# One wide and one narrow matmul per weight tile in the up-projection's paired products, with the halves of a sum added by transfers

## The chip, the cores and the metric

The kernel runs on one core of one Trainium2 chip. The metric is the device time of one execution in microseconds (us), as the median of several runs. The core has five engines that run on their own and meet at semaphores: TensorE (PE, matrix products into PSUM, its weight loads shown apart as PEld), VectorE (DVE), ScalarE (ACT), GpSimd (POOL) and SyncE (SP), which issues most DMA transfers. POOL issues the transfers that add onto their destination.

## The reference

A decoder layer over 512 tokens with 2048 features, all in float32: a token mixer (a recurrent half and an attention half), a layer norm, then a gated MLP with a causal convolution of width 3 over the tokens, then a second layer norm. The part that matters here is the MLP's first half:

```python
x = _layernorm(DEEPNORM_ALPHA * x + mix, ln_mix_g[i], ln_mix_b[i])
hu = _causal_dwconv(jnp.einsum('bsd,df->bsf', x, w_up[i]), ffn_conv_w[i], ffn_conv_b[i])
g, u = jnp.split(hu, 2, axis=-1)                       # 5632 columns each
ffn = jnp.einsum('bsf,fd->bsd', jax.nn.gelu(g) * u, w_down[i])
x = _layernorm(DEEPNORM_ALPHA * x + ffn, ln_ffn_g[i], ln_ffn_b[i])
```

## The kernel before, in words

Features lie on the 128 partitions and tokens along the free dimension, so a product of weights with activations is a sum over tiles of 128 input features. To keep float32 precision with a rounded float32 type (`F32R`), each operand is split into a high part, written by ACT, and a low part, the rest, written by DVE (`split`, lines 106 to 112). A product then needs three matmuls, high x high, high x low and low x high, which all add into one bank (`mm3`, line 114; its matmul is line 117).

The up-projection's 44 column pairs (one tile of g, one of u) are computed in two ways. The first four are plain. The other 40 (class `Pair`, from line 767) use a seven-product scheme: the input features are cut into two halves of eight tiles, the tokens into two halves of 256, and the sums and differences of weights and of activations are formed such that seven products take the place of eight. `PRODUCTS` (line 69) gives their order: p1, p5, p6, p2, p7, p3, p4. Each is a sum over eight tiles of 128 features, of 256 tokens, with three matmuls per tile.

The activation side of the products is built once. `x1[k][h]` holds the normed input of feature tile k and token half h, its high part in the first 256 columns and its low part in the last 256. `forms(j)` (line 727) builds t1 to t4 from sums and differences on POOL, then splits two at a time.

The weight side is loaded per pair. `Pair.before` (line 788) loads four tiles, adds a tile from HBM onto one of them twice with an accumulating transfer (`onto`, line 777, its issue is line 780), adds two sums on DVE (lines 800 and 811) and splits each product's weights two products ahead of its use (lines 110 and 111). `Pair.early` (line 830) copies or adds the finished banks into `cg` and `cu`, 512 columns each: five copies by ACT (lines 835, 838, 840, 845, 850) and three operations by DVE (lines 842, 847, 848). `Pair.late` (line 852) runs the convolution: a scaled copy by ACT (`tap`, line 754), two multiply-adds on DVE (line 748), gelu on ACT (line 862), the product of g and u on DVE (line 866) and a store (line 868).

The loop from line 916 runs one product per step and calls these parts at fixed distances from a pair's first product: a pair's step 0 is its first product, step 6 its last, step 7 the next pair's first. A scheduler then puts each engine's instructions in an order by when their inputs are ready in its own reckoning, so an instruction may stand earlier or later than its call. Tiles come from pools with a fixed number of buffers: `A_BUFS` (62) tiles of 512 columns for all that lives long, `T_BUFS` (12) for the short-lived ones, `RAW_UP` (6) for loaded weights and `W_BUFS` (3) for split ones. Each pair takes three banks of PSUM.

Of the kernel before, what the change touches and what calls it, by code (L numbers as in the profile page):

```python
# [10 lines left out]
F32 = mybir.dt.float32  # L11
F32R = mybir.dt.float32r
AF = mybir.ActivationFunctionType
ALU = mybir.AluOpType
# [33 lines left out]
NC_ = C_LQ + 4 * DH  # L48


A_BUFS = 62
T_BUFS = 12
RAW_BUFS = 3
RAW_UP = 6
# [22 lines left out]
def f32(ap):  # L77
    return ap.bitcast(F32)
# [3 lines left out]
def trunk_kernel(ctx, tc, xT, w_qkg, w_v, gate_w, w_out0, w_out, w_up0, w_up, w_down, consts, out):  # L82
# [11 lines left out]
    def bank():  # L94
        return psum.tile([P, S], F32, tag="ps", bufs=8, name="ps")

    def a_tile(dt=F32R, name="a"):
        return act.tile([P, S], dt, tag="a", bufs=A_BUFS, name=name)

# [6 lines left out]
    def split(src, hi=None, lo=None, mk=a_tile):  # L106

        hi = mk(F32R, "hi") if hi is None else hi
        lo = mk(F32R, "lo") if lo is None else lo
        nc.scalar.activation(hi, src, AF.Copy)  # L110
        nc.vector.tensor_tensor(lo, src, f32(hi), ALU.subtract)  # L111
        return hi, lo

    def mm3(ps, w, x, first, last, onto=False):

        for n, (a, b) in enumerate(((w[0], x[0]), (w[0], x[1]), (w[1], x[0]))):
            nc.tensor.matmul(  # L117
                ps, a, b, start=first and n == 0, stop=last and n == 2, skip_group_check=onto
            )


# [163 lines left out]
    def v_proj(n):  # L285
        pv = [bank() for _ in range(QB)]
        if n == 0:
            load_x(0)
            W.load(1)
            load_x(1)  # L290
            W.load(2)
            load_x(2)
            load_x(3)
            W.load(3)
        for unit in range(KT // 2):
            if n == 0:
                x[2 * unit] = split(x[2 * unit])
            parts = W.take()
            if n + unit == 0:
                parts += W.take()  # L300
            if n == 0:
                x[2 * unit + 1] = split(x[2 * unit + 1])
                load_x(2 * unit + 4)
                load_x(2 * unit + 5)
            for i in range(2):
                kt = 2 * unit + i
                for tt in range(QB):
                    xs = [z[:, tt * P : (tt + 1) * P] for z in x[kt]]
                    mm3(pv[tt], xs, parts[i], kt == 0, kt == KT - 1)
                tick(4 * TK)  # L310
            if n == 0 and unit == 0:
                nc.sync.dma_start(cst, consts)
            if n == 0 and unit == 4:
                constants()
        for tt in range(QB):
            vt[tt] = split(pv[tt])

    def proj():

# [305 lines left out]
    for dt in range(KT):  # L625

        if dt == 3:
            W.hold = True
        if W.hold and not W.raws:
            assert not side  # L630
            early.close()
            W.pool = ctx.enter_context(tc.tile_pool(name="rawu", bufs=1))
            W.bufs, W.hold = RAW_UP, False
            W.load()
        xr = t_tile(F32, "xr")
        nc.sync.dma_start(xr, xT[dt])
        xrs.append(xr)
        if dt == 0:
            continue
        if dt == 1:  # L640
            pair = [bank(), bank()]
            for u in range(KT // 4):
                parts = W.take()
                for kk in range(4):
                    i = 4 * u + kk
                    tick(2 * TK)
                    assert ms[i] is not None
                    hi, lo = parts[kk // 2]
                    for o in range(2):
                        c = slice((kk % 2 * 2 + o) * P, (kk % 2 * 2 + o + 1) * P)  # L650
                        mm3(pair[o], (hi[:, c], lo[:, c]), ms[i], i == 0, i == KT - 1)
            for o in range(2):
                residual(o, pair[o])
            continue
        if dt >= KT - 2:
            wl.append([W.take(), W.take()])
            ys.append(a_tile(F32, "y"))
            continue
        ps = bank()
        for n in range(2):  # L660
            parts = W.take()
            for kk in range(8):
                i = n * 8 + kk
                hi, lo = parts[kk // 4]
                c = slice((kk % 4) * P, (kk % 4 + 1) * P)
                mm3(ps, (hi[:, c], lo[:, c]), ms[i], i == 0, i == KT - 1)
        residual(dt, ps)
# [28 lines left out]
    def sides(z):  # L696
        return z[:, :HALF], z[:, HALF:]
# [29 lines left out]
    def forms(j):  # L727
        a, b = ys[j], ys[j + KT // 2]
        sub = nc.gpsimd.tensor_tensor
        t14, t23 = t_tile(F32, "t14"), t_tile(F32, "t23")  # L730
        (t1, t4), (t2, t3) = sides(t14), sides(t23)
        (b11, b12), (b21, b22) = sides(a), sides(b)
        sub(t1, b12, b11, ALU.subtract)
        sub(t2, t1, b22, ALU.subtract)
        sub(t4, t2, b21, ALU.add)
        sub(t3, b22, b12, ALU.subtract)
        h14, l14 = a_tile(F32R, "hi"), a_tile(F32R, "lo")
        nc.scalar.activation(h14, t14, AF.Copy, scale=-1.0)
        nc.vector.scalar_tensor_tensor(l14, t14, -1.0, f32(h14), ALU.mult, ALU.subtract)
        h23, l23 = split(t23)  # L740
        form["p1", j], form["p2", j] = sides(x1[j][0]), sides(x1[j + KT // 2][0])
        form["p3", j] = sides(x1[j + KT // 2][1])
        form["p5", j], form["p4", j] = zip(sides(h14), sides(l14))
        form["p6", j], form["p7", j] = zip(sides(h23), sides(l23))

    def conv(t, src, ti, *ds):
        for d in ds:
# [19 lines left out]
    class Pair:  # L767
# [49 lines left out]

        def product(self, at):
            if at == 0:
                self.x, self.y, self.z = [bank()[:, :HALF] for _ in range(3)]  # L820
            name = PRODUCTS[at]
            ps = {"p5": self.y, "p3": self.y, "p2": self.z}.get(name, self.x)
            new = name in ("p1", "p5", "p2")
            hi, lo = self.w.pop(name)
            n = KT // 2
            for j in range(n):
                c = slice(j * P, (j + 1) * P)
                mm3(ps, (hi[:, c], lo[:, c]), form[name, j], new and j == 0, j == n - 1, not new)

        def early(self, at):  # L830
            copy, add = nc.scalar.activation, nc.vector.tensor_tensor
            a, b = slice(0, HALF), slice(HALF, S)
            if at == 1:
                self.cg = a_tile(F32, "cg")
                copy(self.cg[:, a], self.x, AF.Copy)
            elif at == 2:
                self.p5 = t_tile(F32, "p5")[:, :HALF]
                copy(self.p5, self.y, AF.Copy)
            elif at == 3:
                copy(self.cg[:, b], self.x, AF.Copy)  # L840
            elif at == 4:
                add(self.cg[:, a], self.cg[:, a], self.z, ALU.add)
            elif at == 5:
                self.cu = a_tile(F32, "cu")
                copy(self.cu[:, b], self.x, AF.Copy, scale=-1.0)
            elif at == 6:
                add(self.cg[:, b], self.cg[:, b], self.y, ALU.add)
                add(self.cu[:, b], self.cu[:, b], self.p5, ALU.subtract)
            elif at == 7:
                copy(self.cu[:, a], self.x, AF.Copy, scale=-1.0)  # L850

        def late(self, at):
            if at == 6:
                self.g = tap(self.cg, 2 * self.i)
                conv(self.g, self.cg, 2 * self.i, 1)
            elif at == 7:
                conv(self.g, self.cg, 2 * self.i, 2)
                self.u = tap(self.cu, 2 * self.i + 1)
            elif at == 8:
                conv(self.u, self.cu, 2 * self.i + 1, 1)  # L860
            elif at == 9:
                nc.scalar.activation(self.g, self.g, AF.Gelu_apprx_tanh)
            elif at == 10:
                conv(self.u, self.cu, 2 * self.i + 1, 2)
            elif at == 11:
                nc.vector.tensor_tensor(self.g, self.g, self.u, ALU.mult)
            elif at == 12:
                nc.sync.dma_start(hidd[self.i], self.g)

    pairs = [Pair(i) for i in range(PLAIN, FT)]  # L870
# [45 lines left out]
    for k in range(last):  # L916
        step(k, "early", 1, 8)
        step(k, "before", -6, 5)
        step(k, "late", 6, 13)
        step(k, "product", 0, NP)  # L920
        ready({last - 5: 4, last - 3: 12, last - 2: 16}.get(k, 0))
        if k == last - 4:
            W.load()
    for k in range(last, last + 6):
        step(k, "early", 1, 8)
        step(k, "late", 6, 13)

    def down_blocks():
        while True:
# [155 lines left out]
```

## Time and profile before

| | |
|---|---|
| median of 3 runs | 2112.58 us (2111.98 to 2113.05) |
| the profiled execution | 2112.73 us |
| its span, first to last instruction | 2111.0 us |
| PE busy | 2076.4 us, 98% |
| DVE, ACT, POOL busy | 63%, 48%, 11% |
| DMA | 286.67 MB, mean 136 GB/s |

The span is what the trace covers; the 1.7 us to the execution's time lie around it. Busy times overlap, since the engines work side by side. PE's busy time counts the pipelined ends of its matmuls too, so how fast it works is read from the distance between starts.

### The profile page before, as it was taken

Reading aid. Unit: us, or ns where it says so; the run is one execution under the profiler, and the core shown is the slowest. Engines: PE = TensorE matmul, PEld = TensorE weight load, DVE = VectorE, ACT = ScalarE, POOL = GpSimd, SP = SyncE. Lnnn points to the kernel's source line nnn. Section 1 sums busy time; section 2 is a strip of 40 time slices with the busy share of each in tenths; the row PEclk is TensorE's granted clock in tenths of the full one; section 3 lists DMA queues with packets and bytes.
Section 4 is the critical chain, followed back from the end, with each engine's and each line's share of the span. In section 5 each row is a group of like instructions: output and inputs, shape, how many; then the busy total and the mean of one; then the engine's idle time right before and its main releaser. Section 6 shows DMA issues by size and latency. Waiting matters only on the chain.

```text
span 2111.0 us, 32632 instructions
## 1 busy us (share of the span) xinstructions
PE 2076.4 (98%) x13035; PEld 1882.6 (89%) x13035; DVE 1334.6 (63%) x2005; ACT 1004.4 (48%) x1644; POOL 240.7 (11%) x289
## 2 busy tenths in 40 slices
PE   9999999999999999999999999999999999999994
PEld 7888888888888899999999999999998888888894
DVE  6576635777335877777777777787776322443368
ACT  4475736666223645555555555555555222322144
POOL 1000000000222340000000000000000000010025
PEclk9999999999999999999999999999999999999997
DMA  6222222222433535666666666666669422333312
GB/s 217 95 80 85 81 95 71 85 98 93 152 118 120 180 86 156 170 167 173 169 175 167 168 175 171 167 175 165 171 163 329 161 93 97 125 110 100 100 50 81
DMA packets 92921, 286.67 MB, mean 136 GB/s; under 512 B 10080, under 2 KB 14176, under 8 KB 92768
## 3 DMA queue, kind: packets, MB, share of 16 engines
q1 hardware_dynamic: 81248, 242.63, 34.5%
q0 software_dynamic: 11520, 41.95, 11.1%
q8 instruction: 102, 1.67, 0.3%
q14 instruction: 51, 0.42, 0.1%
HBM read 264.62 MB, written 19.92 MB: 135 GB/s over the span
## 4 chain that ended last, share of the span: by engine, by line
PE 93%; DVE 4%; ACT 3%; issue 0%; DMA 0%; ACTq 0%; DVEq 0%
PE ps L117 91%; DVE acc L607 1%; PE ps L346 1%; PE ps L347 0%; ACT gt L455 0%; DVE acc L608 0%; PE ps L585 0%; PE ps L376 0%; DVE rstd L604 0%; DVE zs L577 0%; ACT s L358 0%; DVE y L607 0%; DVE y L608 0%; ACT a L461 0%; ACT L473 0%
## 5 line engine op out<-in xcount | busy, mean ns | idle before, releaser
L110 ACT ACTIVATE whi<-raw 128x512 fp32r<-128x512 f32 (+1 forms) x676 | 528.5, 804 | 900.4 <-PE ps L117 812.7
L111 DVE TENSOR_TENSOR wlo<-raw,whi 128x512 fp32r<-128x512 f32 (+1 forms) x676 | 614.3, 925 | 470.5 <-ACT whi L110 468.2
L117 PE MATMUL ps<-hi,whi 128*128 128x512 f32 (+1 forms) x2688 | 910.6, 339 | 0.0
L117 PE MATMUL ps<-hi,wlo 128*128 128x512 f32 (+1 forms) x2688 | 908.1, 338 | 1.2 <-DVE wlo L111 1.2
L117 PE MATMUL ps<-lo,whi 128*128 128x512 f32 (+1 forms) x2688 | 907.6, 338 | 0.0
L117 PEld LDWEIGHTS ps<-hi,wlo 128*128 128x128 f32 x2688 | 510.2, 190 | 56.1 <-DVE wlo L111 2.4
L117 PEld LDWEIGHTS ps<-hi,whi 128*128 128x128 f32 x2688 | 510.3, 190 | 53.1 <-ACT hi L110 0.3
L117 PEld LDWEIGHTS ps<-lo,whi 128*128 128x128 f32 x2688 | 510.4, 190 | 52.8 <-issue 0.5
L117 PE MATMUL ps<-x,whi 128*128 128x256 f32 x2176 | 396.9, 283 | 0.0
L117 PEld LDWEIGHTS ps<-x,whi 128*128 128x128 f32 x2176 | 339.5, 192 | 0.0
L117 PE MATMUL ps<-x,wlo 128*128 128x256 f32 x1088 | 308.0, 283 | 0.0
L117 PEld LDWEIGHTS ps<-x,wlo 128*128 128x128 f32 x1088 | 208.9, 192 | 0.0
L780 POOL DMA_DIRECT2D raw<-in_w_up x80 | 69.2, 964 | 767.8 <-DMA raw<-in_w_up 538.9
L956 POOL TENSOR_TENSOR acc<-acc,shift 128x512 f32<-128x512 f32 x16 | 23.5, 1478 | 437.7 <-ACT shift L566 296.6
L949 DVE SCALAR_TENSOR_TENSOR acc<-acc,ps 128x512 f32<-128x512 f32 x32 | 22.0, 687 | 66.7 <-PE ps L117 66.7
L748 DVE SCALAR_TENSOR_TENSOR cv<-cg,cst,cv 128x511 f32<-128x511 f32 x80 | 59.8, 747 | 1.4
L748 DVE SCALAR_TENSOR_TENSOR cv<-cu,cst,cv 128x511 f32<-128x511 f32 x80 | 59.5, 744 | 0.0
L117 PE MATMUL ps<-x,hi 128*128 128x256 f32 x256 | 49.4, 294 | 5.1 <-DVE x L111 3.3
L117 PE MATMUL ps<-hi 128*128 128x256 f32 (+1 forms) x176 | 51.9, 295 | 0.0
L117 PE MATMUL ps<-lo,hi 128*128 128x256 f32 (+1 forms) x176 | 51.5, 293 | 0.0
L117 PE MATMUL ps<-hi,lo 128*128 128x256 f32 (+1 forms) x176 | 51.5, 293 | 0.0
L800 DVE TENSOR_TENSOR raw<-raw 128x1024 f32<-128x1024 f32 x40 | 49.0, 1226 | 3.1 <-DMA raw<-in_w_up 1.8
(198 smaller groups left out, 1899.8 us busy)
## 6 DMA issues: line engine op xcount, KB each, us to landing
raw<-in_w_up SPq DMA_DIRECT2D x176, 512.0 KB, 4.1
raw<-in_w_down SPq DMA_DIRECT2D x88, 512.0 KB, 3.3
raw<-in_w_up POOLq DMA_DIRECT2D x80, 512.0 KB, 7.1
raw<-in_w_qkg SPq DMA_DIRECT2D x64, 512.0 KB, 3.5
raw<-in_w_out SPq DMA_DIRECT2D x32, 512.0 KB, 3.6
hidd<-cv SPq DMA_DIRECT2D x44, 256.0 KB, 4.2
hid<-hidd SPq DMA_DIRECT2D x44, 256.0 KB, 5.4
raw<-in_w_v SPq DMA_DIRECT2D x15, 512.0 KB, 4.3
```

The lines of the kernel that those rows point to most:

```text
L110: nc.scalar.activation(hi, src, AF.Copy)
L111: nc.vector.tensor_tensor(lo, src, f32(hi), ALU.subtract)
L117: nc.tensor.matmul(ps, a, b, start=first and n == 0, stop=last and n == 2, skip_group_check=onto)
L346: nc.tensor.matmul(ps[:, :L], qs, k[c][:, :L], start=True, stop=False)
L607: sub.tensor_tensor(y, y, self.m[:, tok], ALU.subtract)
L748: nc.vector.scalar_tensor_tensor(t[:, d:], src[:, : S - d], col(C_FW + 3 * ti + 2 - d), t[:, d:], ALU.mult, ALU.add)
L780: nc.gpsimd.dma_start(self.raw[name], w_up[2 * (self.i - 2) + g][:, n * 1024 : (n + 1) * 1024], accum_op=ALU.add,)
L800: add(s2, self.raw["r21"], self.raw["r11"], ALU.add)
L949: nc.vector.scalar_tensor_tensor(acc[dt], acc[dt], 1.0 if c else ALPHA, ps, ALU.mult, ALU.add)
L956: nc.gpsimd.tensor_tensor(acc[d], acc[d], norm2.c, ALU.subtract)
```

## The change

Each product's activation operand is kept as one tile of 512 columns, high part beside low part. `mm2` then issues two matmuls per weight tile in place of three: the high weights over all 512 columns, and the low weights over the first 256. The two column halves of the bank are two parts of one sum. The copies and additions out of the banks take both, so `cg` and `cu` become 1024 columns wide: the sum's first part in columns 0 to 511, the second in 512 to 1023. A transfer from SBUF to SBUF, issued by POOL with addition, adds the second part onto the first, one for `cg` and one for `cu` per pair. The calls of `late` move from steps 6 to 12 to steps 10 to 18. `cg`, `cu` and two tiles of the first norm move to four buffers of 1024 columns of their own, the low parts of the attention values to six buffers of the early pool, and `A_BUFS` goes from 62 to 56. `forms` splits its four sums one by one, each into a tile with both parts.

```diff
-A_BUFS = 62
+A_BUFS = 56
...
+    def mm2(ps, w, x, first, last, onto=False):
+        n = ps.shape[-1] // 2
+        steps = [(ps, w[0], x), (ps[:, :n], w[1], x[:, :n])]
+        for k, (o, a, b) in enumerate(reversed(steps) if last else steps):
+            nc.tensor.matmul(
+                o, a, b, start=first and k == 0, stop=last and k == 1, skip_group_check=onto
             )
...
-            vt[tt] = split(pv[tt])
+            vl = att.tile([P, S], F32R, tag="vl", bufs=6, name="vl")
+            vt[tt] = split(pv[tt], lo=vl)
...
-            ys.append(a_tile(F32, "y"))
+            if dt == KT - 2:
+                last2 = W.pool.tile([P, 2 * S], F32, tag="c", bufs=4, name="y")
+            ys.append(last2[:, :S] if dt == KT - 2 else last2[:, S:])
...
-        h14, l14 = a_tile(F32R, "hi"), a_tile(F32R, "lo")
-        nc.scalar.activation(h14, t14, AF.Copy, scale=-1.0)
-        nc.vector.scalar_tensor_tensor(l14, t14, -1.0, f32(h14), ALU.mult, ALU.subtract)
-        h23, l23 = split(t23)
-        form["p1", j], form["p2", j] = sides(x1[j][0]), sides(x1[j + KT // 2][0])
-        form["p3", j] = sides(x1[j + KT // 2][1])
-        form["p5", j], form["p4", j] = zip(sides(h14), sides(l14))
-        form["p6", j], form["p7", j] = zip(sides(h23), sides(l23))
+        form["p1", j], form["p2", j] = x1[j][0], x1[j + KT // 2][0]
+        form["p3", j] = x1[j + KT // 2][1]
+        for name, t in (("p5", t1), ("p4", t4)):
+            z = form[name, j] = a_tile(F32R, "hl")
+            hi, lo = sides(z)
+            nc.scalar.activation(hi, t, AF.Copy, scale=-1.0)
+            nc.vector.scalar_tensor_tensor(lo, t, -1.0, f32(hi), ALU.mult, ALU.subtract)
+        for name, t in (("p6", t2), ("p7", t3)):
+            form[name, j] = a_tile(F32R, "hl")
+            split(t, *sides(form[name, j]))
...
-                self.x, self.y, self.z = [bank()[:, :HALF] for _ in range(3)]
+                self.x, self.y, self.z = bank(), bank(), bank()
...
-                mm3(ps, (hi[:, c], lo[:, c]), form[name, j], new and j == 0, j == n - 1, not new)
+                mm2(ps, (hi[:, c], lo[:, c]), form[name, j], new and j == 0, j == n - 1, not new)
...
+            two = lambda z: z.rearrange("p (z t) -> p z t", z=2)
+            x, y, z = [two(k) for k in (self.x, self.y, self.z)]
             if at == 1:
-                self.cg = a_tile(F32, "cg")
-                copy(self.cg[:, a], self.x, AF.Copy)
+                self.cg = W.pool.tile([P, 2 * S], F32, tag="c", bufs=4, name="cg")
+                self.g2 = two(self.cg)
+                copy(self.g2[:, :, a], x, AF.Copy)
...
             elif at == 6:
-                add(self.cg[:, b], self.cg[:, b], self.y, ALU.add)
-                add(self.cu[:, b], self.cu[:, b], self.p5, ALU.subtract)
+                add(self.g2[:, :, b], self.g2[:, :, b], y, ALU.add)
+                nc.gpsimd.dma_start(self.cg[:, :S], self.cg[:, S:], accum_op=ALU.add)
+                add(self.u2[:, :, b], self.u2[:, :, b], self.p5, ALU.subtract)
             elif at == 7:
-                copy(self.cu[:, a], self.x, AF.Copy, scale=-1.0)
+                copy(self.u2[:, :, a], x, AF.Copy, scale=-1.0)
+                nc.gpsimd.dma_start(self.cu[:, :S], self.cu[:, S:], accum_op=ALU.add)
...
-            if at == 6:
-                self.g = tap(self.cg, 2 * self.i)
+            if at == 10:
+                self.g = tap(self.cg[:, :S], 2 * self.i)
                 conv(self.g, self.cg, 2 * self.i, 1)
-            elif at == 7:
+            elif at == 11:
                 conv(self.g, self.cg, 2 * self.i, 2)
-                self.u = tap(self.cu, 2 * self.i + 1)
-            elif at == 8:
+            elif at == 12:
+                nc.scalar.activation(self.g, self.g, AF.Gelu_apprx_tanh)
+            elif at == 13:
+                self.u = tap(self.cu[:, :S], 2 * self.i + 1)
+            elif at == 14:
                 conv(self.u, self.cu, 2 * self.i + 1, 1)
...
-        step(k, "late", 6, 13)
+        step(k, "late", 10, 19)
...
-    for k in range(last, last + 6):
+    for k in range(last, last + 12):
```

## Rows read from the trace of the kernel before

**Rows 1.** The page: an engine's busy time and share, the chain's shares.
```profile
PE 2076.4 (98%) x13035; PEld 1882.6 (89%) x13035; DVE 1334.6 (63%) x2005; ACT 1004.4 (48%) x1644; POOL 240.7 (11%) x289
...
PE ps L117 91%; DVE acc L607 1%; PE ps L346 1%; PE ps L347 0%; ACT gt L455 0%; DVE acc L608 0%; PE ps L585 0%; PE ps L376 0%; DVE rstd L604 0%; DVE zs L577 0%; ACT s L358 0%; DVE y L607 0%; DVE y L608 0%; ACT a L461 0%; ACT L473 0%
```

**Rows 2.** Busy time by stretches: length, PE, PEld, DVE, ACT, POOL, clock, DMA share, GB/s.
```profile
790.40:1596.80 806.40, 806.40 (x6708) 805.75 (x6707) 623.50 (x687) 432.46 (x611) 66.41 (x77) 1.00 0.65 172
...
1200.00:1220.16 20.16, 20.16 (x170) 20.16 (x170) 15.54 (x18) 10.70 (x15) 1.73 (x2) 1.00 0.63 168
```

**Rows 3.** Order of time (start, length in us): PE, in a pair, then in the down-projection.
```profile
1204.26 0.28 PE L117 MATMUL ps<-hi,whi 128*128 128x256 f32 x1
...
1207.02 0.28 PE L117 MATMUL ps<-hi,wlo 128*128 128x256 f32 x1
...
1639.70 0.39 PE L117 MATMUL ps<-hi,wlo 128*128 128x512 f32 x1
...
1643.78 0.39 PE L117 MATMUL ps<-hi,wlo 128*128 128x512 f32 x1
```

**Rows 4.** Order of time, PE, where 256 and 512 columns meet.
```profile
235.03 0.28 PE L346 MATMUL ps<-k,q 128*128 128x256 f32 x1
235.15 0.28 PE L347 MATMUL ps<-k,q 128*128 128x256 f32 x1
235.26 0.40 PE L117 MATMUL ps<-hi,whi 128*128 128x512 f32 x1
235.50 0.40 PE L117 MATMUL ps<-lo,whi 128*128 128x512 f32 x1
...
1593.06 0.40 PE L117 MATMUL ps<-hi,whi 128*128 128x512 f32 x1
1593.30 0.40 PE L117 MATMUL ps<-lo,whi 128*128 128x512 f32 x1
```

**Rows 5.** Groups by shape: busy us, mean ns of one, idle before and releaser.
```profile
L840 ACT ACTIVATE cg<-ps 128x256 f32<-128x256 f32 x40 | 14.6, 366 | 0.0
...
L455 ACT ACTIVATE gt<-ps,cst 128x512 f32<-128x512 f32 x16 | 10.1, 686 | 1.9 <-PE ps L117 1.9
...
L842 DVE TENSOR_TENSOR cg<-cg,ps 128x256 f32<-128x256 f32 x40 | 16.8, 421 | 25.9 <-PE ps L117 25.9
...
L866 DVE TENSOR_TENSOR cv<-cv 128x512 f32<-128x512 f32 x40 | 27.7, 692 | 1.4
```

**Rows 6.** Order of time, DVE and ACT, end of one pair.
```profile
1231.35 1.23 DVE L111 TENSOR_TENSOR wlo<-raw,whi 128x1024 fp32r<-128x1024 f32 x1 [0.55 <-ACT whi L110]
...
1234.43 0.62 ACT L862 ACTIVATE cv<-cv 128x512 f32<-128x512 f32 x1
```

**Rows 7.** POOL in order of time; DMA from 900 to 1500; line 780's landing.
```profile
1229.99 0.86 POOL L780 DMA_DIRECT2D raw<-in_w_up  x1 [18.43 <-DMA raw<-in_w_up]
1231.68 0.85 POOL L780 DMA_DIRECT2D raw<-in_w_up  x1 [0.83 <-issue]
...
q0 software_dynamic: 8604, 31.38, 29.2%
...
raw<-in_w_up POOLq DMA_DIRECT2D x60, 512.0 KB, 8.0
...
DMA to landing us min/median/max: 5.2/8.0/11.5
```

**Rows 8.** Stretches of one product each from a pair's begin, columns as in 2.
```profile
1212.90:1215.78 2.88, 2.88 (x26) 2.88 (x25) 2.54 (x4) 2.56 (x4) 0.00 (x0) 1.00 0.95 188
...
1221.54:1224.42 2.88, 2.88 (x26) 2.88 (x25) 2.01 (x2) 1.33 (x2) 0.00 (x0) 1.00 0.25 87
```

**Rows 9.** Waits (total us, times, longest): building the forms, line 800, reloaded tiles.
```profile
POOL t L733 <- DMA hidd<-cv: 4.4, 1, 4.4
...
DVE raw L800 <- DMA raw<-in_w_up: 1.8, 3, 1.2
ACT hi L110 <- DMA hid<-hidd: 1.4, 3, 0.8
```

More of the change, by code (lines that the diff above doesn't have):

```diff
@@ L118, in mm3 @@
                 ps, a, b, start=first and n == 0, stop=last and n == 2, skip_group_check=onto
+            )
+    def mm2(ps, w, x, first, last, onto=False):
[4 more added lines that the diff above has]
+                o, a, b, start=first and k == 0, stop=last and k == 1, skip_group_check=onto
             )
@@ L833, in early @@
             if at == 1:
-                self.cg = a_tile(F32, "cg")
-                copy(self.cg[:, a], self.x, AF.Copy)
+                self.cg = W.pool.tile([P, 2 * S], F32, tag="c", bufs=4, name="cg")
+                self.g2 = two(self.cg)
+                copy(self.g2[:, :, a], x, AF.Copy)
             elif at == 2:
-                self.p5 = t_tile(F32, "p5")[:, :HALF]
-                copy(self.p5, self.y, AF.Copy)
+                self.p5 = two(t_tile(F32, "p5"))
+                copy(self.p5, y, AF.Copy)
@@ L839, in early @@
             elif at == 3:
-                copy(self.cg[:, b], self.x, AF.Copy)
+                copy(self.g2[:, :, b], x, AF.Copy)
             elif at == 4:
-                add(self.cg[:, a], self.cg[:, a], self.z, ALU.add)
+                add(self.g2[:, :, a], self.g2[:, :, a], z, ALU.add)
             elif at == 5:
-                self.cu = a_tile(F32, "cu")
-                copy(self.cu[:, b], self.x, AF.Copy, scale=-1.0)
+                self.cu = W.pool.tile([P, 2 * S], F32, tag="c", bufs=4, name="cu")
@@ L846, in early @@
+                self.u2 = two(self.cu)
+                copy(self.u2[:, :, b], x, AF.Copy, scale=-1.0)
             elif at == 6:
-                add(self.cg[:, b], self.cg[:, b], self.y, ALU.add)
-                add(self.cu[:, b], self.cu[:, b], self.p5, ALU.subtract)
+                add(self.g2[:, :, b], self.g2[:, :, b], y, ALU.add)
+                nc.gpsimd.dma_start(self.cg[:, :S], self.cg[:, S:], accum_op=ALU.add)
+                add(self.u2[:, :, b], self.u2[:, :, b], self.p5, ALU.subtract)
@@ L857, in late @@
                 conv(self.g, self.cg, 2 * self.i, 2)
-                self.u = tap(self.cu, 2 * self.i + 1)
-            elif at == 8:
+            elif at == 12:
[3 more added lines that the diff above has]
+            elif at == 14:
                 conv(self.u, self.cu, 2 * self.i + 1, 1)
-            elif at == 9:
-                nc.scalar.activation(self.g, self.g, AF.Gelu_apprx_tanh)
-            elif at == 10:
+            elif at == 15:
@@ L864, in late @@
                 conv(self.u, self.cu, 2 * self.i + 1, 2)
-            elif at == 11:
+            elif at == 17:
                 nc.vector.tensor_tensor(self.g, self.g, self.u, ALU.mult)
-            elif at == 12:
+            elif at == 18:
                 nc.sync.dma_start(hidd[self.i], self.g)
@@ L923, in trunk_kernel @@
             W.load()
-    for k in range(last, last + 6):
+    for k in range(last, last + 12):
         step(k, "early", 1, 8)
-        step(k, "late", 6, 13)
+        step(k, "late", 10, 19)
     def down_blocks():
```

## The prediction

> **What bounds the kernel now.** I read the page's engine totals and its chain first: TensorE (PE) is busy for 98% of the span, and 91% of the chain that ended last is the matmuls of line 117 [rows 1]. Next the stretch of the 40 pairs, 790.4 to 1596.8 us, in the table by stretches: PE busy 806.40 of 806.40 us at granted clock 1.00 (the upper of its two levels, 2.4 GHz), DVE 623.50, ACT 432.46, DMA share 0.65 [rows 2]. Nothing in this stage ends a wait of PE's; it is bound by how fast matmuls follow each other, and a shorter matmul stream shortens it one for one until another engine catches up.
>
> So the next view is PE's order of time. In a pair, the 256-column matmuls start 120 ns apart: 23 steps from 1204.26 to 1207.02, 2.76 us [rows 3]. In the down-projection 512-column matmuls start 226.7 ns apart: 18 steps from 1639.70 to 1643.78, 4.08 us [rows 3]. Doubling the columns adds 106.7 ns, and 120 less 106.7 leaves 13.3 ns that each matmul costs whatever its width. That is what the change can win: it keeps the columns and makes fewer matmuls.
>
> **The change, part by part.** *Matmuls.* A block is one 128x128 weight tile of one product. Before: three matmuls of 256 columns, 3 x 120 = 360 ns. After: one of 512 (high weights over high and low halves of x1, which lie side by side) and one of 256, 226.7 + 120 = 346.7 ns. There are 40 pairs x 7 products x 8 = 2240 blocks: 2240 x 13.3 ns = 29.9 us less. A product goes from 2.88 to 2.77 us, a pair from 20.16 to 19.41. The trace has no steady alternation of 512 and 256; the nearest rows are transitions. Two 256s between 512s: 235.03, 235.15, 235.26, then 235.50, so 0.47 us for two 256s and a 512, where 2 x 0.120 + 0.2267 gives 0.467 [rows 4]. After the long run of 256s the first 512 takes 0.24 us, from 1593.06 to 1593.30 [rows 4]. I take no surcharge, from the first, which is nearest to an alternation; at the other end 13 ns a block, all of the gain. A gain beyond 30 us would need a 512 after a 256 below 226.7 ns, and no row of mine shows one.
>
> The Trainium skill speaks against this size: "TensorE: Matmul & The Clock Gate", section "Back-to-back issue gap", gives a warm matmul N/2.4 + 2.5 ns, so 2.5 ns to win per matmul and, as an estimate, 5.6 us in all. The rows disagree: 120 and 226.7 ns, not 109 and 216.
>
> *Emptying the banks.* The bank now holds two parts side by side, so five ACT copies and three DVE operations per pair go from 256 to 512 columns. ACT: 366 ns now [rows 5]; at 512 columns 686 ns from a bank (the sigmoid), so 5 x 0.32 = 1.6 us more: 10.70 [rows 2] becomes 12.3 of 19.41. DVE: 421 ns now, 692 for two 512-column inputs (line 866) [rows 5], 3 x 0.27 = 0.8 more: 15.54 becomes 16.3 of 19.41, 84%. Neither is the bound. Their cover is that each bank has a whole product, 2.77 us, before PE writes it again, and a copy takes 0.7. The splits of weights run two products ahead: the split done at 1232.58 (line 111 on DVE, 1231.35 + 1.23) [rows 6] feeds the product that starts at 1235.94 (the pair begins at 1212.90). Slack 3.4 us, some 3.15 with the shorter products. While ACT or DVE lose less than that at one go, PE does not see it. Value 0.
>
> *Adding the two parts.* Two accumulating transfers per pair, 80 in all, 256 KB each, issued by POOL. POOL's issues take 0.86 us each [rows 7] and POOL does nothing else in the pairs (1.73 us of 20.16 [rows 2]); now 3.5 of 19.41. On its queue they stand behind the two that add onto the weights (1229.99 and 1231.68, that is 5.93 and 6.52 products after the pair's begin); the sum for g is ready only at about 6.5, when the third operation is done, so g's comes last at 6.8 and u's at 7.5, and each of the others waits at most 0.86 us more for its turn. On the DMA engines: the software queue took 29.2% of 600 us for 60 transfers of 512 KB, 2.92 us of all 16 engines each [rows 7]. A 256 KB one costs 1.46 (by bytes) to 2.92 us (by rows of 128). The DMA share of a pair goes from 0.65 x 20.16 = 13.1 us to 16.0 to 18.9 of 19.41, 83 to 98%; I take the first, since the lines are half as long and none comes from HBM. The share by products shows where the room is: 0.95 in product 0, 0.25 in product 3 [rows 8]; the new transfers come at the start of the full stretch and land at its end.
>
> *The wait.* The first tap of g (ACT, line 754) is called at step 10 and now waits for its transfer. The transfer runs in one queue behind the second weight addition, whose kind lands after 5.2, 8.0 (median) or 11.5 us [rows 7]. Its issue at 6.52 steps is 18.1 us from the pair's begin with the new products; it lands at 26.1 (median) to 29.6; plus 1.46 to 2.92: g's sum is there 27.5 to 32.5 us after the begin. Step 10 begins at 27.7, and the split that stands ahead of the tap ends at about 28.9. So the tap waits 0 to 3.6 us, at the median landing none. Behind it on ACT stand the split of the next weights and a copy of a bank; behind its convolution on DVE, the other half of that split. PE waits for those two, with 3.15 us of slack. Value 0; bound 0.45 us a pair, 18 us. u's tap has six steps instead of four.
>
> *Buffers.* 56 long-lived tiles instead of 62: 24 of x1 and 32 formed ones fill them exactly during the pairs, while cg and cu move to four tiles of their own. While the forms are built some must wait for a tile; POOL waits 4.4 us for one already [rows 9]. Value 0, since PE is then at the plain products and needs the forms only after them; bound 5 us. The last pairs' convolutions end some eight products later; their hidden tiles are read in the last chunk, hundreds of us on.
>
> Sum: profiled execution 2112.7 us, span 2111.0; the 1.7 us around the span stay, and the execution lies 0.15 us above the median of the runs. 2112.7 - 29.9 = 2083 us.
>
> **The rivals.** *A: the tap is put in too early (slower).* Instructions don't stand in the order of the code: gelu is called at step 9 and runs at 1234.43, step 7.5 [rows 6]. If ACT's order counts on a quicker landing, g's tap may stand right behind the split and the copy of step 8, at 8.4 steps or 23.3 us. It then waits 4.2 to 9.2 us, at the median landing 4.2 to 5.7, and holds up ACT and, through the convolution, DVE. Less the slack, PE loses 1.1 to 2.6 us a pair, 42 to 102 us: 2125 to 2185. It turns slower where the wait exceeds 3.15 + 0.75 = 3.9 us (30 us over 40 pairs). For it: that reordering. Against it: elsewhere the order agrees with the landings; ACT waited only 1.4 us for reloaded hidden tiles, and DVE 1.8 us in 40 pairs for line 800, which reads an added-onto tile [rows 9].
>
> *B: no fixed cost is saved.* If every 512 behind a 256 costs 0.24 us, as the first ones after a change of width do [rows 4], a block takes 360 ns as before and nothing is gained: 2113. Against it: the sum over two 256s and a 512 above. The rule of the Trainium skill named above ("TensorE: Matmul & The Clock Gate", "Back-to-back issue gap") comes out near this, at an estimated 2107.
>
> *C: DMA becomes the bound.* If a 2 KB line from SBUF costs twice a 4 KB line of a weight addition, the two transfers take 11.7 us and a pair needs 24.8 us of DMA: over 2290 us. Nothing in the trace points there, but it has no transfer from SBUF into SBUF.
>
> **How the numbers follow.** The forecast, 2083 (2079 to 2106 with the bounds of the wait and of the buffers): 0.58. A: 0.28, of which 0.07 where part of the gain is left or it is just eaten up. B: 0.05. C: 0.04. Some other part of the gain lost, without turning slower: 0.05. The range is 2079 to 2140: above it lies C and the dearer part of A, some 0.18. This kernel's time can tell 0.2%, 4 us, from no change: faster by more 0.64 (the forecast, 0.04 of A, 0.02 of the rest), within 0.11 (0.03 of A, B, 0.03 of the rest), slower 0.25 (0.21 of A, C).
>
> **What would show it.** Right: in the pairs, 512- and 256-column starts that alternate 0.227 and 0.120 us; 19.4 us from one pair to the next; PE busy all through, DVE near 84%, DMA share 0.80 to 0.85; g's tap near step 10 with no wait worth the name. A would show as ACT's line 754 waiting for a DMA on cg, then PE waiting for line 111. B as a 512 of 0.24 us. C as weight loads that land later and later. I am wrong if PE has gaps in the pairs, or if a block is not 347 ns.

## The result, and the profile after

The changed kernel takes 2264.38 us (2253.56 to 2267.91) against 2112.28: a ratio of 1.0711 [1.0675, 1.0747], slower by 152 us where 30 us less was forecast. The page of the kernel after: engines, then the chain by engine and by line.

```profile
PE 2115.0 (93%) x10795; PEld 1799.2 (80%) x10795; DVE 1362.3 (60%) x2021; ACT 1049.9 (46%) x1660; POOL 308.8 (14%) x369
...
PE 56%; DMA 18%; issue 12%; DVE 8%; ACT 3%; POOL 2%; ACTq 0%; POOLq 0%; SPq 0%; DVEq 0%
PE ps L117 49%; DMA cu<-cu 10%; DMA raw<-in_w_up 7%; PE ps L127 6%; DVE wlo L111 2%; POOL raw L795 1%; DVE x L111 1%; DVE acc L618 1%; DVE cg L867 1%; ACT cg L859 1%; DVE cv L763 0%; PE ps L357 0%; ACT gt L466 0%; PE ps L358 0%; DVE acc L619 0%
```

The chain of before was nearly all matmuls [rows 1]; now 18% of it is DMA, and the transfer for u alone (cu onto cu) is 10%. The table by stretches, over the pairs (columns as in [rows 2]):

```profile
800.00:1700.00 900.00, 808.43 (x4310) 692.82 (x4308) 611.24 (x650) 449.52 (x572) 132.22 (x152) 0.94 0.67 168
```

PE is idle for 91.6 of these 900 us and has a mean granted clock of 0.94. Where the time lies is read from one instruction that each pair has once, the first copy of a bank. Its group before (line 835) and after (line 854), with the first and the last start:

```profile
L835 ACT ACTIVATE cg<-ps x40: 362/365/367, 793.5 to 1579.7; 128x256 f32<-128x256 f32 x40
```
```profile
L854 ACT ACTIVATE cg<-ps x40: 598/599/601, 800.9 to 1715.8; 128x512 f32<-128x512 f32 x40
```

A pair takes (1715.8 - 800.9) / 39 = 23.46 us instead of 20.16: 128.7 us more. The first pair is 7.4 us later, and from the last copy to the end it takes 2263.0 - 1715.8 = 547.2 us instead of 531.3: 15.9 more. Together 152.0, the difference of the two spans. All runs below are read by these three numbers.

The waits in the pairs that bear on PE, from the list of waits (800 to 1710 us; each line: who waits <- for whom: total us, times, longest):

```profile
ACT cv L769 <- DMA cu<-cu: 157.7, 38, 6.1
PEld ps L127 <- ACT cg L859: 106.3, 38, 4.7
PE ps L127 <- ACT cg L859: 94.1, 37, 4.4
...
DVE raw L815 <- DMA raw<-in_w_up: 40.7, 23, 3.1
```

Line 769 is the tap, line 859 the copy that empties p6's bank for p7, line 127 the matmul of the new products. One such case in order of time, ACT first, then PE:

```profile
1202.77 0.81 ACT L769 ACTIVATE cv<-cg,cst 128x512 f32<-128x512 f32 x1 [0.52 <-DMA cg<-cg]
1209.36 0.81 ACT L769 ACTIVATE cv<-cu,cst 128x512 f32<-128x512 f32 x1 [5.78 <-DMA cu<-cu]
1210.08 0.57 ACT L859 ACTIVATE cg<-ps 128x512 f32<-128x512 f32 x1
```
```profile
1205.91 0.39 PE L127 MATMUL ps<-x,whi 128*128 128x512 f32 x1
1210.71 0.80 PE L127 MATMUL ps<-hl,whi 128*128 128x512 f32 x1 [4.41 <-ACT cg L859]
...
1211.52 0.63 PE L127 MATMUL ps<-hl,whi 128*128 128x512 f32 x1
...
1214.72 0.61 PE L127 MATMUL ps<-hl,whi 128*128 128x512 f32 x1
```

u's tap is called at step 13, g's at step 10; the order on ACT has them next to each other, both ahead of the copy of step 10 (step 3 of the next pair). u's tap waits 5.78 us, the copy stands behind it, and PE behind the copy. After these 4.41 us without a matmul the five blocks from 1211.52 to 1214.72 start 0.64 us apart, where a block takes 0.353 us in a stretch at granted clock 1.00. The row of these blocks (columns as in [rows 2]) has a granted clock of 0.50, the lower of the two levels, 1.2 GHz:

```profile
1211.52:1214.72 3.20, 3.20 (x12) 2.71 (x11) 3.08 (x4) 1.27 (x3) 0.00 (x0) 0.50 0.23 56
```

Idle time (91.6 us) and lower clock (6% of 900, by estimate 54 us) make 146 us, and 39 x (23.46 - 19.74) = 145 is what the pairs take over a full PE (19.74 is measured below).

The transfers' issues on POOL for this pair:

```profile
1194.92 1.14 POOL L868 DMA_DIRECT2D cg<-cg  x1
1195.46 1.49 POOL L795 DMA_DIRECT2D raw<-in_w_up  x1
1196.00 1.82 POOL L872 DMA_DIRECT2D cu<-cu  x1
```

g's is done 7.8 us after its issue, u's, behind the second addition onto weights in the same queue, 13.4 us after, when its tap starts (medians from issue to landing: 7.9 and 11.5 us).

### The profile page after: what moved, and what is told of

The parts are those of the page before. It is cut to its first block, busy times and chain, and to the rows that moved or that the text cites. A ratio compares the mean times of both kernels' runs of the same rounds, so it can differ in the third digit from the quotient of the medians.

```text
span 2263.0 us, 28449 instructions
## 1 busy us (share of the span) xinstructions
PE 2115.0 (93%) x10795; PEld 1799.2 (80%) x10795; DVE 1362.3 (60%) x2021; ACT 1049.9 (46%) x1660; POOL 308.8 (14%) x369
## 4 chain that ended last, share of the span: by engine, by line
PE 56%; DMA 18%; issue 12%; DVE 8%; ACT 3%; POOL 2%; ACTq 0%; POOLq 0%; SPq 0%; DVEq 0%
PE ps L117 49%; DMA cu<-cu 10%; DMA raw<-in_w_up 7%; PE ps L127 6%; DVE wlo L111 2%; POOL raw L795 1%; DVE x L111 1%; DVE acc L618 1%; DVE cg L867 1%; ACT cg L859 1%; DVE cv L763 0%; PE ps L357 0%; ACT gt L466 0%; PE ps L358 0%; DVE acc L619 0%
## 5 line engine op out<-in xcount | busy, mean ns | idle before, releaser
L127 PE MATMUL ps<-hl,whi 128*128 128x512 f32 x1280 | 500.0, 426 | 94.2 <-ACT cg L859 94.1
L117 PE MATMUL ps<-hi,wlo 128*128 128x512 f32 (+1 forms) x1408 | 546.8, 388 | 10.2 <-DVE wlo L111 10.2
L117 PE MATMUL ps<-hi,whi 128*128 128x512 f32 (+1 forms) x1408 | 549.3, 390 | 3.6 <-ACT whi L110 3.6
L117 PE MATMUL ps<-lo,whi 128*128 128x512 f32 (+1 forms) x1408 | 546.0, 388 | 0.0
L127 PEld LDWEIGHTS ps<-hl,whi 128*128 128x128 f32 x1280 | 257.0, 203 | 155.8 <-ACT cg L859 106.3
L127 PE MATMUL ps<-hl,wlo 128*128 128x256 f32 x1280 | 351.2, 295 | 0.0
L127 PE MATMUL ps<-x,whi 128*128 128x512 f32 x960 | 349.8, 398 | 0.0
L117 PEld LDWEIGHTS ps<-hi,wlo 128*128 128x128 f32 x1408 | 265.0, 188 | 66.6 <-DVE wlo L111 12.5
L117 PEld LDWEIGHTS ps<-hi,whi 128*128 128x128 f32 x1408 | 265.1, 188 | 56.7 <-ACT whi L110 4.3
L127 PEld LDWEIGHTS ps<-hl,wlo 128*128 128x128 f32 x1280 | 261.1, 204 | 13.9
```

The costliest lines, as they stand in the source:

```text
L117: nc.tensor.matmul(ps, a, b, start=first and n == 0, stop=last and n == 2, skip_group_check=onto)
L127: nc.tensor.matmul(o, a, b, start=first and k == 0, stop=last and k == 1, skip_group_check=onto)
```

## The experiments

Theory W: what costs is ACT waiting at u's tap for the transfer. Theory L: the transfers load DMA so much that the weights come late. Later two more questions came up: what is lost ahead of the pairs, and why the block is dearer than forecast.

**Transfers that nobody reads.** Each adds the other way round, so no tap waits for it.

```diff
-nc.gpsimd.dma_start(self.cg[:, :S], self.cg[:, S:], accum_op=ALU.add)
+nc.gpsimd.dma_start(self.cg[:, S:], self.cg[:, :S], accum_op=ALU.add)
```

(and the same for cu)

> The 80 transfers stay, with their size, queue and time of issue, but add the first part onto the second, which nobody reads; so no tap waits for one (the output leaves out the products with the low half of x1). Theory W (ACT stands at u's tap and waits for the landing): the changed kernel's PE gaps in the pairs go, a pair takes 19.8 us (56 blocks of about 0.3535 us as the gap-free stretches of the changed kernel show) and the whole about 2105 us (2095 to 2120), since some 7 us ahead of the pairs stay. Theory L (the load of the transfers on DMA engines and POOL delays the weight loads): stays above 2200 us.

Measured 2148.42 us, 1.0168 [1.0151, 1.0185]; a pair every 20.57 us. Between both expectations: 116 us go with the tap's wait, but a load effect is left. Its waits, 800 to 1560 us:

```profile
DVE raw L815 <- DMA raw<-in_w_up: 100.9, 32, 4.6
...
PE ps L127 <- DVE wlo L111: 22.9, 26, 1.8
```

Line 815 adds the weights up and waits for an addition that now lands behind a transfer; the splits (line 111) come later by it, and PE waits for them.

**No transfers at all.** Both lines are deleted.

> The 80 transfers are left out (the output leaves out the products with the low half of x1). Both theories: about 2105 us (2095 to 2120). The difference to the kernel whose transfers nobody reads is the price of their load alone: W expects under 5 us, L over 90 us. The block of one 512 and one 256 column matmul can be read here without gaps: 0.347 us if the prediction's sum was right, 0.3535 us as read in the changed kernel.

2114.12 us, 1.0002 [0.9992, 1.0011]; a pair every 19.74 us, PE never idle in the pairs. The load alone, that is unread transfers against none, costs 34 us, where W had expected under 5 and L over 90. The pairs without transfers:

```profile
800.00:1560.00 760.00, 760.00 (x4314) 660.93 (x4313) 604.60 (x650) 452.95 (x577) 65.51 (x76) 1.00 0.66 173
```

So 39 x (20.16 - 19.74) = 16.4 us are all that the larger matmuls can give, and this kernel, which has nothing to wait for, gives them back: its first copy is at 802.9 instead of 793.5, and its end 9.4 us longer.

**All late calls four steps later** (14 to 22 instead of 10 to 18).

> The convolution's calls four steps later still (14 to 22). Theory W with a scheduler that goes by its own reckoning of the landing: both taps stand where they stood in ACT's order, next to each other ahead of the fourth copy, and the time stays at 2264 us (2230 to 2290). Rival (the call decides the place): the taps come after the landing, about 2105 us.

2130.66 us (one run), which neither expectation had; it lies nearer to the rival's. The later call moves u's tap by a whole pair, while g's still stands ahead of the copy of step 10; a pair takes 20.10 us, no tap waits long in them (1.5 us at most), line 815 waits 79.2 us, the first copy is at 793.8, but the end takes 551.1 us.

**Taps pinned.** Both taps are queued on ACT behind the split of the step at which they are called.

```diff
-self.u = tap(self.cu[:, :S], 2 * self.i + 1)
+with tc.issue_after(behind[0]):
+    self.u = tap(self.cu[:, :S], 2 * self.i + 1)
```

(and g's; `behind[0]` is the ACT instruction of the last split)

> The changed kernel with one thing added: on ACT each tap is queued behind the split of the weights of its own step (10 for g, 13 for u), issue order only. g's transfer lands by 10.3 steps, u's by 12.4, as the changed kernel's landings of at most 9.7 and 13.3 us show. Theory W: no wait of note is left, 2105 us (2095 to 2125). Theory L: still over 2200 us.

2107.86 us, 0.9979 [0.9969, 0.9988]: 156 us less with every transfer kept. A pair takes 19.74 us and PE is full:

```profile
800.00:1560.00 760.00, 760.00 (x4315) 660.93 (x4314) 616.74 (x652) 451.99 (x575) 131.73 (x152) 1.00 0.81 199
```

W holds. Line 815 still waits 35.5 us in 38 times here, 2.5 us at most, and PE doesn't see it. So the load of L need not cost anything; which slack it meets here and not in the unread run was not taken apart.

**Only u's tap pinned.**

> The kernel after, all transfers kept; of the two taps only u's is queued on ACT behind the split of the step at which it is called, g's stays where the scheduler likes it. Theory W, with u's tap as the culprit (its waits for the transfer were 160 us in all, g's 14 us): nearly all of what pinning both gave comes back, 2105 to 2125 us, and the waits of PE for the bank copy of line 861 here are gone. Rival: g's early tap is what displaces the copy, or takes u's place as the long wait: over 2180 us.

2108.29 us, 0.998 [0.997, 0.999], 19.74 us a pair: u's tap was all of the pairs' loss.

**Only the buffers**, on the kernel before: 56 long-lived tiles, six of their own for the low halves of v, cg and cu in four double tiles.

> The kernel before with only the change's buffers: 56 instead of 62 of the large pool, six of its own for the low halves of v, and cg, cu and the last two residual tiles in four tiles of twice the size. Products, parts and calls are those of before. If the 7 to 9 us that most variants lose ahead of the first pair (first bank copy at 801 to 803 us against 793.5) come from the buffers: 2118 to 2124 us, first bank copy at about 801. If from the order in which the scheduler places the later steps: 2112 us, first bank copy at 793.5. The prediction priced the buffers at nothing, with a bound of 5 us.

2121.32 us, 1.0035 [1.0023, 1.0047]; first copy at 801.7, pairs and end as before. The 8 us ahead of the pairs belong to the buffers. DVE, POOL and PE at that place:

```profile
737.94 9.80 DVE L111 TENSOR_TENSOR x<-y,x 128x256 fp32r<-128x256 f32 x1 [2.12 <-ACT x L110]
...
736.93 1.00 POOL L739 TENSOR_TENSOR t<-y 128x256 f32<-128x256 f32 x1
737.63 0.99 POOL L737 TENSOR_TENSOR t<-t,y 128x256 f32<-128x256 f32 x1
...
746.59 0.86 POOL L738 TENSOR_TENSOR t<-t,y 128x256 f32<-128x256 f32 x1
...
747.79 0.58 PE L117 MATMUL ps<-x,hi 128*128 128x256 f32 x1 [5.85 <-DVE x L111]
```

One subtraction of DVE, the last but one of the splits of x1, takes 9.80 us instead of 0.42, as long as POOL computes the differences for the forms one behind the other; PE waits 5.85 us for it and then runs some 3 us at its lower level (granted clock 0.54 from 747.79 to 751.00). In the kernel before the splits are over (last start 731.7) when POOL begins its differences (734.95). The group of these splits (min, median, max), before and here:

```profile
L111 DVE TENSOR_TENSOR x<-y,x x32: 405/412/943, 684.5 to 731.7; 128x256 fp32r<-128x256 f32 x32
```
```profile
L111 DVE TENSOR_TENSOR x<-y,x x32: 410/416/9800, 687.7 to 747.7; 128x256 fp32r<-128x256 f32 x32
```

All runs with a first copy after 800 us have one split of 9.0 to 12.0 us, the kernel after too (9.83); in the others none is over 1.05.

Late splits beside POOL's stream are not always held, though. The run with the calls four steps later has both (DVE, then POOL), and its longest split takes 1.05 us; POOL's differences start 0.87 us apart beside its last splits, and 0.69 us apart in the run with only the buffers:

```profile
738.28 1.39 DVE L111 TENSOR_TENSOR x<-y,x 128x256 fp32r<-128x256 f32 x2 [1.06 <-ACT x L110]
```
```profile
738.49 0.90 POOL L746 TENSOR_TENSOR t<-y 128x256 f32<-128x256 f32 x1
739.36 0.91 POOL L748 TENSOR_TENSOR t<-t,y 128x256 f32<-128x256 f32 x1
740.23 0.73 POOL L747 TENSOR_TENSOR t<-t,y 128x256 f32<-128x256 f32 x1
```

The times of the run with only the buffers point the same way: two of its eight executions took 2113.0 and 2113.7 us, the other six 2120.9 to 2123.2. No trace of a short one was kept, and what decides which of the two engines is held stays open.

**The same with the differences on DVE**, which takes POOL's stream away.

```diff
-        sub = nc.gpsimd.tensor_tensor
+        sub = nc.vector.tensor_tensor
```

> The kernel before with the change's buffers, as in the run that lost 8 us, and with the differences for the forms computed on DVE instead of POOL. If the long subtraction is DVE held up beside POOL's stream: no split of x1 over 1.1 us, first bank copy at 793 to 796 us, 2112 to 2116 us. If the scarcity of buffers itself delays PE there, whoever computes the differences: 2120 us or more, and another instruction waits.

2113.44 us, 1.0004 [0.9995, 1.0013]; first copy at 794.0, and with the splits as late as in the run before (they begin at 687.7 in both) none is long:

```profile
L111 DVE TENSOR_TENSOR x<-y,x x32: 415/422/959, 687.7 to 738.0; 128x256 fp32r<-128x256 f32 x32
```

So the change's buffers make the splits late, and POOL's stream beside them can make one of them dear.

**The kernel after with both mended**: taps pinned and the differences on DVE, all transfers and buffers kept.

> The kernel after, all its transfers and buffers kept, with both taps queued behind their step's split (the pinned run, 2107.9 us) and the differences on DVE. If the two causes add up: the first bank copy comes 5 to 8 us earlier than 800.9, pairs every 19.74 us, 2099 to 2103 us. If the long subtraction was not the cause: 2108 again.

2098.00 us, 0.9931 [0.9917, 0.9945]. First copy 793.9 (+0.4), 39 pairs at 19.74 us (-16.4), end 534.2 us (+2.9): -13.1, the difference of the spans (2097.9 and 2111.0). The two causes and the block account for the kernel after, but for 2.9 us at the end.

**Parts added by an engine, calls still late**: the two transfers become additions on DVE, or on POOL (`add` is `nc.vector.tensor_tensor`; the same for cu).

```diff
-nc.gpsimd.dma_start(self.cg[:, :S], self.cg[:, S:], accum_op=ALU.add)
+add(self.cg[:, :S], self.cg[:, :S], self.cg[:, S:], ALU.add)
```

> The kernel after with the two parts added on DVE from SBUF to SBUF (128x512) in place of the two transfers; the calls of the taps stay late. No transfer, so no long wait at a tap wherever it is queued: 2100 to 2116 us, a pair every 19.74 us as in the run without transfers, if DVE (16.1 of 20 us busy in the pinned run, and some 1.4 us more per pair for two additions of 0.69 us) keeps up. Theory L has nothing against it, since the DMA share falls to 0.66. Rival: DVE at some 17.5 of 19.7 us is late with the weights' low halves often enough to stop PE, over 2125 us.

> The same with the two additions on POOL. POOL is nearly idle in this stage but for issuing transfers. If an addition there costs DVE nothing: 2100 to 2112 us. If POOL's additions slow DVE's (the two reading SBUF side by side) or hold up the issue of the weight additions queued behind them on POOL: DVE waits at line 815 as in the run with unread transfers, 2115 to 2150 us.

On DVE 2118.39 us, 1.0021 [1.0010, 1.0031], above its expectation; on POOL (`nc.gpsimd.tensor_tensor`) 2116.38, 1.0014 [1.0005, 1.0024], in the range of the dearer case but not for its reason, since line 815 waits only 2.2 us there. Both have 19.74 us a pair with a full PE, both lose 8 to 9 us ahead of the pairs and have an end of 545.4 and 543.3 us.

**Parts added by an engine, calls at the old steps**, 60 long-lived tiles, no tiles of their own for v, two double tiles for cg and cu: on DVE with calls at 6 to 12, on DVE with the taps one step later, on POOL with the taps one step later.

> The parts added on DVE, the taps called at the steps of the kernel before (6 to 12), and the buffers nearly given back: 60 of the large pool, none of their own for v, two double tiles in place of four. The gain of the block is 16 us in every run with a full PE. If the loss ahead of the pairs came from the six missing buffers and the loss behind them (14 us in the run with DVE additions and late calls) from the late calls: first bank copy at about 795 us, 2096 to 2103 us, faster than before by 0.5 to 0.8%. If 60 buffers are still too few and the end is set by something else: 2110 to 2118. Rival: an early tap now waits on ACT for DVE's addition in the same step, and PE stops at the bank copy behind it as with the transfers: over 2130.

> The same with both taps called one step later (7 and 8), so that DVE's addition lies a step ahead of the tap. If taps that wait in order on ACT cost anything in the run with calls at 6 and 7, it is gone here: 2094 to 2100 us. If nothing waits there, both come out within 2 us of each other.

> As the one before, with both additions on POOL (1.59 us each there against 0.68 on DVE), which takes 1.4 us per pair from DVE but puts POOL's additions ahead of the weight additions' issue. Within 3 us of the run on DVE if DVE was not what PE waits for; 3 to 8 us faster if DVE's load set the end; slower if POOL's additions stretch DVE's (DVE was busy 175 of 200 us with the additions on POOL against 172 with them on DVE itself): 2105 to 2115.

2104.75 (0.9961 [0.9948, 0.9975]), 2103.91 (0.9957 [0.9945, 0.9970]) and 2098.39 us (0.9935 [0.9923, 0.9948]). First copies at 794.3, 792.1 and 793.4: with 60 tiles nothing is lost there. The end is 538.9, 538.9 and 532.3 us, so 6.5 and 11.0 us of it are the late calls or the buffers, which these runs change together; the run with only the buffers had lost nothing there (531.5 us), which speaks for the calls. With the additions on DVE 7.6 us of the end stay, and by them the first two came out above their expectation; POOL's version is 5.5 us faster, as expected for the case that DVE's load sets the end.

**Order of the widths in a product**, on the version with POOL's additions: seven matmuls of 512, eight of 256, one of 512; and in twos (512, 256, 256, 512, 512, ...). The order in twos ran twice, the second time for its profile: of the first five executions the profiled one took 4504.89 us, with PE's matmuls twice as far apart throughout and a granted clock of 1.00 in its rows, for a reason that is not known, and the other four 2089.86 to 2091.92.

```diff
-            for j in range(n):
...
+            for m, (k, j) in enumerate(todo):
...
-                mm2(ps, (hi[:, c], lo[:, c]), form[name, j], new and j == 0, j == n - 1, not new)
+                nc.tensor.matmul(
+                    ps[:, :h] if k else ps, (hi, lo)[k][:, c],
+                    form[name, j][:, :h] if k else form[name, j],
+                    start=new and m == 0, stop=m == 2 * n - 1, skip_group_check=not new,
+                )
```

(`todo` lists high or low weights, k, and the block, j, in the new order)

> The version with POOL's additions, but inside each product of eight blocks the matmuls are put by width: seven of 512 columns, then eight of 256, then the last of 512; two changes of width per product in place of 14. If a change costs some 6.5 ns (the surplus of 0.3525 over 0.3467 us, 5.8 ns a block, on 14 changes per 8 blocks is 3.3 ns; at 1.75 changes a block): a pair takes 56 x 0.3467 + 14 x 0.0033 = 19.46 us instead of 19.77, 12 us less over 40 pairs, 2086 us. If the columns themselves are slower in this stage, or the order costs nothing: 19.75 us a pair, 2098 us.

> The same with two matmuls of a width next to each other (512, 256, 256, 512, 512, ...): eight changes of width per product. If the change of width is what costs, about half of the grouped run's gain: 19.6 us a pair, 2092 us. If not: 2098 us, as the version with POOL's additions.

> The order in twos once more, for its profile. By its time, 1.5 us under the grouped run, a pair every 19.55 us (grouped: 19.59, POOL version: 19.77) if the difference lies in the pairs; 19.75 if it lies elsewhere.

Grouped 2091.47 us (0.9899 [0.9885, 0.9914]), in twos 2089.90 (0.9896 [0.9879, 0.9912]) and 2091.33 us (0.9897 [0.9881, 0.9914]). These beat both kernels; against the version with POOL's additions grouping won 7 us where 12 were expected, the order in twos 7 to 8 where 6 were. Grouped, then in twos, the first copies:

```profile
L859 ACT ACTIVATE cg<-ps x40: 571/575/598, 792.3 to 1556.2; 128x512 f32<-128x512 f32 x40
```
```profile
L859 ACT ACTIVATE cg<-ps x40: 572/576/600, 794.1 to 1556.2; 128x512 f32<-128x512 f32 x40
```

19.59 and 19.54 us a pair, against 19.77 alternating. The order matters, but with 2, 8 and 14 changes of width per product the surplus over 56 x 0.3467 = 19.41 us is 0.17, 0.13 and 0.35 us: no fixed price per change.

**Only 512 columns in the pairs**, on the version with POOL's additions: the low weights, too, go over all 512 columns.

```diff
-        steps = [(ps, w[0], x), (ps[:, :n], w[1], x[:, :n])]
+        steps = [(ps, w[0], x), (ps, w[1], x)]
```

> The version with POOL's additions with every matmul of the pairs 512 columns wide (the low half of the weights goes over the low half of x1 too, a product that the reference's precision doesn't need). No change of width in the stage. If 512 columns take there what they take in the down-projection (0.2267 us): 56 x 0.4534 = 25.39 us a pair and about 2098 + 40 x 5.6 = 2323 us. If they take 0.2286 us as in the grouped run: 25.60 us a pair, about 2331 us. If they are as slow as in the alternating blocks (0.2355): 26.4 us a pair, about 2362 us.

2324.75 us (one run). Its first copies:

```profile
L852 ACT ACTIVATE cg<-ps x40: 573/591/601, 794.5 to 1784.5; 128x512 f32<-128x512 f32 x40
```

(1784.5 - 794.5) / 39 = 25.385 us, over 112 matmuls 0.2267 us each, as in the down-projection [rows 3]. The 512 columns are not slower in this stage, and 256 alone took 120 ns there in the kernel before [rows 3]; so it is the mixing of the widths that costs.

## Why the prediction was wrong

*Matmuls: right in kind, mis-sized.* The prediction's block of 346.7 ns measured 352.5 (19.74 / 56), so 7.5 ns a block are won, 16.8 us in all, not 13.3 and 29.9. Both single rates were right (0.2267 and 0.120); the failed choice was "no surcharge", taken from one sequence of two 256s between 512s [rows 4]. That is the order in twos, where a block takes 349 ns, and not the alternation that the change makes. Rival B, a 512 of 0.24 us, had 13 ns; 6 are real. The formula of the Trainium skill that the prediction sets against its size ("TensorE: Matmul & The Clock Gate", section "Back-to-back issue gap") is given there for a matmul by itself, and for a stream the page has other spacings; the 2.5 ns that it leaves to win per block are not what was measured either.

*Emptying the banks: right.* In the pinned run DVE takes 616.74 / 760 of 19.74 = 16.0 us a pair (16.3 forecast), ACT 11.7 (12.3), and PE sees neither.

*Adding the parts: right in load.* DMA share 0.81 pinned against 0.66 without transfers, times 19.74, is 3.0 us for two transfers: some 1.5 each, as the lower end that was taken (1.46), and rival C fell. What the step left out is what the transfers do to their neighbours in the queue: line 815 waits. On its own, unread, that cost 0.83 us a pair.

*The wait: this step failed.* g's tap, which was worked out, did wait next to nothing (13.9 us in 18 times over all pairs). u's was dismissed in one sentence, "u's tap has six steps instead of four". It was given the step of its call, but it stood three steps earlier; its transfer queues behind a weight addition as well, and lands last. Behind it on ACT stands, ahead of any split, the copy that empties the bank p7 needs, and it has not the 3.15 us of slack that were counted: of 5.78 us of wait, 4.41 reached PE. Value 0 and bound 18 us against 145 measured.

*Rival A had the mechanism and too low a price.* "The tap is put in too early", 0.28, 2125 to 2185 us. It priced g's tap, with the split's slack, and left out the clock: by estimate 54 of the 146 us are matmuls at the lower level after the gaps. Why the order on ACT puts u's tap ahead of its call was not taken apart.

*Buffers: this step failed too.* "Value 0, since PE is then at the plain products" looked at who waits for a tile, not at what runs beside what. The splits of x1 that PE still needs slid under POOL's differences; 8 us, above the bound of 5, wherever one of them was held. The Trainium skill, "SBUF — State Buffer", sections "Who interferes with whom" and "Summary: rules for kernel authors", says that a DVE instruction with two inputs in SBUF contends with a GpSimd instruction that reads SBUF, and that the second one to issue blocks until the first finishes. The trace agrees that they contend (9.80 us, and 0.42 with POOL's stream gone); it differs on how long: 13 further instructions of POOL's began while DVE was held, from 738.33 to 746.59, so the block lasted through many instructions and not one.

*The end* was passed over ("their hidden tiles are read in the last chunk, hundreds of us on"): 15.9 us in the kernel after, 3 with the taps pinned. PE's waits from the last first copy to the end, in the kernel after:

```profile
PE ps L117 <- DVE wlo L111: 9.0, 2, 8.4
...
PE ps L117 <- ACT whi L110: 3.6, 1, 3.6
```

These 12.6 us at the beginning of the down-projection have no counterpart before: its first weights' splits (lines 110 and 111) stand on ACT and DVE among the last pair's taps and convolutions, and the taps wait 3.38 and 2.38 us for their transfers. With the taps pinned PE waits 2.6 us for splits there. But without transfers it still waits 7.1 us, and with DVE's additions and late calls 10.8, so the transfers are not all of it. The buffers alone left the end at 531.5 us; that leaves the late calls and the order in which they are put, though no run changed only the calls back. With the calls at the old steps and the additions on DVE it is 5.1 us.

## What to carry to other kernels

Where an instruction comes to wait for a transfer, find out where the queue of its engine will really hold it, and price what stands behind it there, PE's lower clock after each gap included; the transfer that lands last is the one to work out, not the first. When buffers are taken away, ask what slides in time and beside which engine's stream it then runs. A rate between two matmul widths is to be read from the very order in which they will stand.

## What the runs showed of the hardware

One DVE subtraction of 128x256 was held for 9.80 us (0.42 alone) beside an unbroken stream of POOL operations of 0.9 us each; in another run such subtractions took 1.05 us at most beside the same stream, and POOL's starts moved apart instead. A 512-column and a 256-column matmul in alternation take 352.5 to 353 ns, grouped 350, in twos 349, where each width by itself takes 226.7 and 120; what the surplus of 2 to 6 ns consists of stays open. An accumulating transfer of 256 KB from SBUF to SBUF takes some 1.5 us of all 16 DMA engines, about half of the 2.92 us of a 512 KB one from HBM [rows 7].
